# Attention's values as the stationary operand, in two parts side by side, with the transposed probabilities moving in two parts

## The chip, the cores and the metric

The kernel runs on one core of a Trainium2 chip. The metric is the device time of one execution in microseconds (us), and the median of several executions is compared. The core's engines run side by side, each in its own program order: TensorE (PE; its weight loads are listed apart as PEld), VectorE (DVE), ScalarE (ACT), GpSimd (POOL), and SyncE (SP), which here only issues transfers. They wait for one another by semaphores. On-chip memory is SBUF; TensorE writes to PSUM, in banks of 128 partitions x 512 float32 values.

## What is computed

One layer of a decoder trunk for 1024 tokens of width 1024: a spatial gating unit on one half of the projected columns, sparse attention on the other half (8 query heads of 64 in 2 groups, one key/value head for each group), an output projection `w_out` and a feed-forward part. In attention an indexer scores all earlier keys, the best 256 for each query are kept, and the change concerns what is done with them:

```
score = sum_h w_idx * relu(q_idx . k_idx)          # causal
_, idx = top_k(score, 256);  kg, vg = k[idx], v[idx]
logits = einsum('btkgd,btjkd->btkgj', qg, kg) / 8
p = softmax(logits)                                 # float32
o = einsum('btkgj,btjkd->btkgd', p, vg)
merged = concat(RMSNorm(y_a), RMSNorm(o));  x += gate * RMSNorm(merged @ w_out)
```

## The kernel before, in words

Tokens stand in 8 blocks of 128. The kernel doesn't gather keys: a mask `BI` with a large number at each key that is not kept is added to the logits of all causal keys, so query block b works on b+1 key blocks.

Most large products work in three terms: a float32 operand is split into a high part in a replicated float32 format (F32R in the code, fp32r in the trace) and a low part, the difference, in the same format. `split_w` does this for weights: ScalarE copies (and scales, L224) the high part, and VectorE (L225) or GpSimd (L222) subtracts it for the low part. `q_stack` (L391, L392) and `merge_T` (L712, L713) do it for transposed queries and for the merged rows. Products in plain F32 need no split: the transposes against `ident`, and before the change the product of probabilities and values.

The program has stages. Stage 2 projects keys, values and the indexer's vectors for each block; the values are copied by ScalarE from PSUM into `VV` (L377). Then come the indexer's scores `SC`, the gating unit (tiles `gvb`, `WM`, `vn`, `ya` in the pool `up`, together with `uv`, which the masks later use too), and the search for each query's threshold: `select(b)` is a serial chain on VectorE (L603, L605, L607), whose last step `more` (L650) releases a small matmul (L652) and, behind it on TensorE, the remaining query projections.

Attention runs over 32 units (b, group, pair of heads), blocks in the order 0, 7, 1, 6, 5, 4, 3, 2, four units for each. For unit u the loop writes, in this order: `logits(u+1)`: for each of the two heads and each chunk of up to 512 keys two matmuls (L730), one VectorE step that adds the mask and takes the minimum (L731), and one ScalarE exponential (L734) into `L`. Then `values(u)`: for each pair of key blocks (a "chunk"; 80 in all) four 128x128 transposes of `L` into one PSUM bank (`probs_T`, L769), one ScalarE copy to SBUF (`pT`, 128x512 or, for a single key block, 128x256; L750), and for each key block and head a matmul (L755) with the transposed probabilities (128x128) stationary and the 64 columns of `VV` moving. Each such matmul leaves two records in the trace. After the second pair `normed` multiplies the bank by the reciprocal of the softmax sums (L779, L780) into `yb`. Then a mask where one is due (`MASKS`: blocks 6, 5, 4, 3, 2 at units 4, 6, 8, 9, 10; block 7's before), `stack_for` the queries of unit u+3, and, four units behind, `finish` (RMSNorm of `yb`, L785, L787, and its `merge_T`). At unit 14 the first half of `w_out` is loaded through the two buffers `raw` of the pool `rp` (L207) and split; from unit 19 on, each odd unit runs `oproj0`, 24 matmuls (L807 to L809) for one finished block. adaLN sums (L481) run between on VectorE.

A scheduler decides each engine's order from the order of the code, priorities, and estimated readiness; the compiled program fixes it. Pools are stacks: memory of a pool that is closed is given to the next one, whose first writers wait for the last users.

## Time and profile before

| | us |
|---|---|
| three runs | 1246.74, 1246.16, 1245.63 (median 1246.16) |
| the profiled execution, its own time | 1248.28 |
| its span, first to last instruction | 1246.4 |
| TensorE busy in the span | 1164.5 (93%) |
| VectorE, ScalarE, GpSimd busy | 873.8, 671.2, 209.4 |
| attention, from block 7's first logits to its end | 345.5 to 546 |
| the mean granted clock of TensorE | 0.967 of full speed |

The profile is one execution. The busy shares tell which engine is full on the whole; windows tell it for a stretch; the timeline lists instructions with their starts, and the difference between two starts in a full stretch is what an instruction really takes (matmuls overlap, so their lengths are longer than their pace). A wait is given as who waited for whom.

### The profile page before, as it was taken

The page shows a single profiled execution, that of the slowest core. Times are in us where ns is not written, and L with a number is a line of the kernel's source. Part 1 is how long each engine was busy: PE and PEld are TensorE (multiplying, and loading weights), DVE is VectorE, ACT ScalarE, POOL GpSimd, SP SyncE. Part 2 cuts the span into 40 slices and gives each one's busy share as a digit, 9 for nine tenths or more (in the row PEclk, how much of TensorE's full clock was granted, in tenths as well). Part 3 has the DMA queues.
Part 4 walks back from the last instruction along what each step waited for, and adds up shares of the span by engine and source line. Part 5 has one row for each costly group of instructions (what it writes and reads, how often), then busy time and mean ns, then how long its engine had stood idle before and what let it go on. Part 6 is the DMA issues. An engine that isn't in the chain of part 4 may idle for free.

```text
span 1246.4 us, 16883 instructions
## 1 busy us (share of the span) xinstructions
PE 1164.5 (93%) x5785; PEld 985.0 (79%) x5785; DVE 873.8 (70%) x1798; ACT 671.2 (54%) x1410; POOL 209.4 (17%) x304
## 2 busy tenths in 40 slices
PE   4899989995898999899899999999999999999997
PEld 4887768884697999887687788888887888888886
DVE  7844998968478666627898775655558756876568
ACT  4554679773266755537735455555544454445452
POOL 3585605451100000012610000000000000000001
PEclk9899989996898999999999999999999999999999
DMA  9431102110000144446315753544458455533335
GB/s 343 150 93 35 52 1 64 52 64 9 1 10 29 57 161 161 172 149 215 115 60 195 269 178 127 169 143 145 161 217 331 125 188 179 197 91 99 102 98 205
DMA packets 80239, 162.41 MB, mean 130 GB/s; under 512 B 7724, under 2 KB 32920, under 8 KB 80152
## 3 DMA queue, kind: packets, MB, share of 16 engines
q1 hardware_dynamic: 80136, 161.33, 38.3%
q8 instruction: 45, 0.74, 0.3%
q14 instruction: 42, 0.34, 0.1%
q10 hardware_dynamic: 16, 0.00, 0.0%
HBM read 119.36 MB, written 41.94 MB: 129 GB/s over the span
## 4 chain that ended last, share of the span: by engine, by line
PE 51%; DVE 12%; issue 4%; DMA 3%; ACT 2%; POOL 1%; SPq 0%; DVEq 0%; POOLq 0%; ACTq 0%
PE tr L1174 8%; PE lg L1174 8%; PE mm L1174 5%; PE mm L755 4%; PE lg L991 2%; PE lg L993 2%; PE lg L992 2%; PE tr L769 2%; PE lg L730 2%; PE tr L991 2%; PE tr L993 2%; PE tr L992 2%; DVE w L882 2%; PE mm L991 1%; PE mm L993 1%
## 5 line engine op out<-in xcount | busy, mean ns | idle before, releaser
L881 ACT ACTIVATE w<-rx 128x512 fp32r<-128x512 f32 x112 | 70.7, 632 | 148.1 <-PE lg L1174 64.5
L1174 PE MATMUL tr<-w,w 128*128 128x512 f32 x504 | 134.3, 392 | 2.9 <-DVE w L882 2.9
L1174 PE MATMUL lg<-w,w 128*128 128x512 f32 x504 | 133.7, 390 | 0.0
L882 DVE TENSOR_TENSOR w<-rx,w 128x512 fp32r<-128x512 f32 x112 | 77.2, 689 | 57.8 <-ACT w L881 57.1
L301 PE MATMUL mm<-w,hT 128*128 128x512 f32 (+1 forms) x288 | 112.8, 393 | 4.7 <-ACT hT L293 3.5
L1174 PEld LDWEIGHTS tr<-w,w 128*128 128x128 f32 x504 | 95.4, 189 | 23.2 <-DVE w L882 3.4
L303 PE MATMUL mm<-w,hT 128*128 128x512 f32 (+1 forms) x288 | 111.2, 387 | 0.0
L304 PE MATMUL mm<-w,hT 128*128 128x512 f32 (+1 forms) x288 | 110.2, 384 | 1.0 <-POOL hT L294 1.0
L1174 PEld LDWEIGHTS lg<-w,w 128*128 128x128 f32 x504 | 94.9, 188 | 19.7
L1210 POOL TENSOR_TENSOR rsf<-rsf,mhalf 128x1 f32<-128x1 f32 x8 | 6.0, 752 | 605.6 <-DVE rsf L1209 605.6
L1174 PE MATMUL mm<-w,w 128*128 128x512 f32 x336 | 93.9, 389 | 0.0
L755 PEld LDWEIGHTS mm<-VV,pT 128*128 128x128 f32 x576 | 76.1, 199 | 3.8 <-ACT pT L750 1.6
L755 PE MATMUL mm<-VV,pT 128*128 128x64 f32 x576 | 76.4, 277 | 0.9 <-ACT pT L750 0.9
L1174 PEld LDWEIGHTS mm<-w,w 128*128 128x128 f32 x336 | 63.1, 188 | 13.2
L882 DVE TENSOR_TENSOR w<-b,w 128x512 fp32r<-128x512 f32 x96 | 65.7, 685 | 4.0 <-ACT w L881 4.0
L301 PEld LDWEIGHTS mm<-w,hT 128*128 128x128 f32 x288 | 55.8, 194 | 14.9 <-ACT hT L293 3.7
L730 PE MATMUL lg<-KS,qs 128*128 128x512 f32 (+5 forms) x192 | 55.3, 399 | 10.6 <-DVE mxs L731 6.0
L882 DVE TENSOR_TENSOR w<-s,w 128x512 fp32r<-128x512 f32 x56 | 38.2, 688 | 37.3 <-ACT w L881 37.3
L304 PEld LDWEIGHTS mm<-w,hT 128*128 128x128 f32 x288 | 55.0, 191 | 10.5 <-POOL hT L294 1.3
L734 ACT ACTIVATE L<-L,mxs 128x128 f32<-128x128 f32 (+7 forms) x64 | 49.2, 771 | 25.8 <-DVE mxs L731 25.6
L881 ACT ACTIVATE w<-b 128x512 fp32r<-128x512 f32 x96 | 59.4, 618 | 6.7 <-DMA b<-in_w_ff_dram 6.5
L303 PEld LDWEIGHTS mm<-w,hT 128*128 128x128 f32 x288 | 55.5, 193 | 8.5
(356 smaller groups left out, 2975.5 us busy)
## 6 DMA issues: line engine op xcount, KB each, us to landing
rx<-x_scratch SPq DMA_DIRECT2D x56, 512.0 KB, 3.5
x_scratch<-d SPq DMA_DIRECT2D x108, 256.0 KB, 3.0
ada<-in_w_ada_dram SPq DMA_DIRECT2D x48, 512.0 KB, 5.6
raw<-in_w_ff_dram SPq DMA_DIRECT2D x32, 512.0 KB, 4.1
b<-in_w_ff_dram SPq DMA_DIRECT2D x32, 512.0 KB, 4.6
x<-in_x_dram SPq DMA_DIRECT2D x16, 512.0 KB, 5.6
raw<-in_w_in_dram SPq DMA_DIRECT2D x8, 512.0 KB, 3.6
raw<-in_w_in_dram SPq DMA_DIRECT2D x16, 256.0 KB, 2.8
```

The lines of the kernel that those rows point to most:

```text
L301: mm = T.matmul(p[:, :n], lh, wt[k][:, 0, :n], start=k == 0, stop=False)
L303: T.matmul(p[:, :n], lh, wt[k][:, 1, :n], start=False, stop=False)
L304: T.matmul(p[:, :n], ll, wt[k][:, 0, :n], start=False, stop=k == KD - 1)
L730: T.matmul(pl, QS[b, grp][:, q, h4 * P:(h4 + 1) * P], KS[:, grp, c0:c0 + cw], start=q == 0, stop=q == 1)
L734: ex = A.activation(L, L, AF.Exp, scale=-1.0, bias=top, accum_out=sms[:, b, h:h + 1])
L755: mm = T.matmul(po[:, o:o + 64], e[:, (si * 2 + h2) * P:(si * 2 + h2 + 1) * P], VV[:, s0 + si, grp], start=first, stop=pair == 1 and s0 + ...
L881: A.activation(hi, src, AF.Copy)
L882: eng.tensor_tensor(lo, src, hi.bitcast(F32), op=OP.subtract)
L991: ms.append(T.matmul(p, a[:, 0, k], b[:, 0, k], start=start and k == 0, stop=False, skip_group_check=more))
L992: ms.append(T.matmul(p, a[:, 0, k], b[:, 1, k], start=False, stop=False, skip_group_check=more))
L993: ms.append(T.matmul(p, a[:, 1, k], b[:, 0, k], start=False, stop=stop and k == 3, skip_group_check=more))
L1174: ms.append(T.matmul(p, x[:, qa, t * P:(t + 1) * P], y[:, qb], start=start and n == 0, stop=stop and n == 2, skip_group_check=more))
```

## The change

Four things change; the new lines are numbered as in the file after.

1. **The product.** `VV` holds each head's 64 values twice side by side: the high part and the low part, both F32R (ScalarE copies the first, a new VectorE subtraction the second, eight times in stage 2). In `values` these 128 columns are now the stationary operand, and the transposed probabilities move: 256 columns (two heads) at a time, once their high part and once their low part. A key block and unit now take two matmuls (L768) where they took two of another shape with two records each. The result is transposed (rows: high-part and low-part outputs; columns: queries).
2. **The low part of the probabilities.** ScalarE's copy from PSUM gives the high part. The low part is subtracted by VectorE from PSUM (L764; 46 chunks), or, where `on_pool` says so (34 chunks), ScalarE copies the bank a second time into a `raw` buffer of `rp` (L759, L760) and GpSimd subtracts (L761).
3. **Back to rows.** `values_T` copies a block and group's bank to SBUF (ScalarE, `oT`, 16 times), transposes it with four TensorE transposes (L787), and `normed` first adds the two parts (a VectorE reduction from 512 to 256 elements, L806), then multiplies (L807, in place of L780). It is called one unit later, and `finish` moves one unit later too.
4. **Memory.** Two temporaries of the rotary tables reuse one buffer each; the gating unit's tiles get a pool `gp` that closes after the query projections; the probabilities' tiles take its place (pool `pe`) and from unit 13 on lie in the pool `op`, over `SC`. `mxs` loses a dimension: the first chunk's minimum is kept in `sms`.

```diff
-    VV = mid.tile([P, NB, 2, 64], F32, name="VV")
+    VV = mid.tile([P, NB, 2, P], F32R, name="VV")
...
-        A.activation(VV[:, j], vv, AF.Copy)
+        A.activation(VV[:, j, :, 0:64], vv, AF.Copy)
+        V.tensor_tensor(VV[:, j, :, 64:128], vv, VV[:, j, :, 0:64].bitcast(F32), op=OP.subtract)
...
-    gvb = up.tile([P, 512], F32, name="gvb")
+    gp_stack, gp = push("gp")
+    gvb = gp.tile([P, 512], F32, name="gvb")
...
+    gp_stack.close()
+    pe_stack, pe_pool = push("pe")
+    pe = [pe_pool]
...
-        po = PO[b, grp]
+        po = PO[b, grp][:, pair * 256:pair * 256 + 256]
...
-            e = p2.tile([P, 512], F32, tag="pT", name=nm("pT"), bufs=2)
             wd = cnt_s * 256
-            A.activation(e[:, :wd], pt[:, :wd], AF.Copy)
+            e = pe[0].tile([P, 2, 512], F32R, tag="pT", name=nm("pT"), bufs=2)
+            hi, lo = e[:, 0, :wd], e[:, 1, :wd]
+            if on_pool(u, s0):
+                r = rp.tile([P, 2, 512], F32, tag="raw", name=nm("pr"))[:, 0, :wd]
+                A.activation(r, pt[:, :wd], AF.Copy)
+                A.activation(hi, pt[:, :wd], AF.Copy)
+                G.tensor_tensor(lo, r, hi.bitcast(F32), op=OP.subtract)
+            else:
+                A.activation(hi, pt[:, :wd], AF.Copy)
+                V.tensor_tensor(lo, pt[:, :wd], hi.bitcast(F32), op=OP.subtract)
             for si in range(cnt_s):
-                for h2 in range(2):
-                    o = (pair * 2 + h2) * 64
...
-                    mm = T.matmul(po[:, o:o + 64], e[:, (si * 2 + h2) * P:(si * 2 + h2 + 1) * P], VV[:, s0 + si, grp],
-                                  start=first, stop=pair == 1 and s0 + si == ns - 1 and h2 == 1)
+                for q in range(2):
...
+                    mm = T.matmul(po, VV[:, s0 + si, grp], e[:, q, si * 256:si * 256 + 256], start=first,
+                                  stop=pair == 1 and s0 + si == ns - 1 and q == 1)
...
-        if pair == 1:
-            normed(yb_of(b)[:, grp * 256:grp * 256 + 256].rearrange("p (h e) -> p h e", h=4),
-                   po[:, :256].rearrange("p (h e) -> p h e", h=4), b, grp * 4, 4)
+
+    def on_pool(u, s0):
+        b = units[u][0]
+        if b < 2:
+            return False
+        return (s0 // 2) % 2 == 0 if b > 5 else s0 == 0 if b == 5 else u % 4 < 2
+
+    def values_T(b, grp):
+
+        oT = p2.tile([P, 512], F32, tag="yb", name=nm("oT"), bufs=3)
+        A.activation(oT, PO[b, grp], AF.Copy)
+        p = p_tr()
+        for i in range(4):
+            T.transpose(p[:, i * P:(i + 1) * P], oT[:, i * P:(i + 1) * P], ident)
+        normed(yb_of(b)[:, grp * 256:grp * 256 + 256].rearrange("p (h e) -> p h e", h=4),
+               p.rearrange("p (h w e) -> p h e w", h=4, w=2), b, grp * 4, 4)
...
         V.reciprocal(sms[:, b, h:h + n], sms[:, b, h:h + n])
-        V.tensor_tensor(dst, src, sms[:, b, h:h + n, None].to_broadcast([P, n, 64]), op=OP.mult)
+        V.tensor_reduce(dst, src, op=OP.add, axis=mybir.AxisListType.X)
+        V.tensor_tensor(dst, dst, sms[:, b, h:h + n, None].to_broadcast([P, n, 64]), op=OP.mult)
...
+        if u and u % 2 == 0:
+            values_T(*units[u - 1][:2])
         values(u)
         if u in MASKS:
             mask(MASKS[u])
         if u == 12:
+            pe_stack.close()
             u_stack.close()
             sc_stack.close()
             o_stack, op_ = push("op")
+            pe[0] = op_
...
-        if u % 4 == 0 and u:
+        if u % 4 == 1 and u > 1:
             finish(OB[u // 4 - 1])
...
+    values_T(OB[-1], 1)
     finish(OB[-1])
```

VectorE in stretch A, from the mask of block 4's end into block 3's; before (the names: `self`, `seli`, `eq` belong to the mask, `mT` is the merged rows, `L` the logits):

```order
L671 CAST seli_2643<-self_2642 128x1
L674 SCALAR_TENSOR_TENSOR seli_2643<-seli_2643 128x1
L676 TENSOR_TENSOR self_2642<-seli_2643,self_2642 128x1
L680 TENSOR_SCALAR BI,self_2642<-SC,self_2642 128x512
L713 TENSOR_TENSOR mT_4154<-tr_4270,mT_4154 128x4x128
L681 TENSOR_SCALAR eq_4306<-SC,self_2642 128x512
L683 TENSOR_SCALAR self_2642<-self_2642 128x1
L731 ISA L_4324,mxs<-lg_4325,BI 128x256
```

After, at the mask of block 3 (lines are shifted by some 5: L679 is the former L674, L681 L676, L685 L680, L686 L681, L688 L683, L718 L713, L822 L795):

```order
L806 TENSOR_REDUCE yb_4424<-tr_4419 128x256
L718 TENSOR_TENSOR mT_4220<-tr_4398,mT_4220 128x4x128
L679 SCALAR_TENSOR_TENSOR seli_2657<-seli_2657 128x1
L764 TENSOR_TENSOR pT_4434<-tr_4429,pT_4434 128x512
L822 TENSOR_SCALAR ya_4452<-ya_4452,rsa 128x512
L807 TENSOR_TENSOR yb_4424<-yb_4424,sms 128x256
L681 TENSOR_TENSOR self_2656<-seli_2657,self_2656 128x1
L685 TENSOR_SCALAR BI,self_2656<-SC,self_2656 128x512
L686 TENSOR_SCALAR eq_4375<-SC,self_2656 128x512
L688 TENSOR_SCALAR self_2656<-self_2656 128x1
L718 TENSOR_TENSOR mT_3147<-tr_4458,mT_3147 128x4x128
```

Between the steps of the same mask now stand a subtraction (L764), a reduction (L806) and the product with the sums (L807).

ScalarE where the first half of `w_out` is scaled; before:

```order
L750 ACTIVATE pT_4463<-tr_4458 128x512
L734 ACTIVATE L_4493,sms<-L_4493,mxs 128x896
L750 ACTIVATE pT_4472<-tr_4469 128x256
L224 ACTIVATE wo_4642<-raw_4640,cols 128x512
L224 ACTIVATE wo_4645<-raw_4640,cols 128x512
L224 ACTIVATE wo_4650<-raw_4648,cols 128x512
L224 ACTIVATE wo_4653<-raw_4648,cols 128x512
L712 ACTIVATE mT_3122<-tr_4486 128x4x128
```

After:

```order
L759 ACTIVATE pr_4746<-tr_4740 128x512
L760 ACTIVATE pT_4745<-tr_4740 128x512
L763 ACTIVATE pT_4757<-tr_4754 128x256
L717 ACTIVATE mT_4220<-tr_4768 128x4x128
L224 ACTIVATE wo_4777<-raw_4775,cols 128x512
L224 ACTIVATE wo_4780<-raw_4775,cols 128x512
L224 ACTIVATE wo_4785<-raw_4783,cols 128x512
L224 ACTIVATE wo_4788<-raw_4783,cols 128x512
L224 ACTIVATE wo_4793<-raw_4791,cols 128x512
L224 ACTIVATE wo_4796<-raw_4791,cols 128x512
L759 ACTIVATE pr_4833<-tr_4827 128x512
```

Four scalings of two loads stood in a row and the other four came one pair at a time; now six of three loads stand in a row, directly behind a chunk whose second copy `pr` takes a `raw` buffer, and ahead of the next one.

TensorE in stretch B, in block 5's values; before:

```order
L755 MATMUL mm_4896<-VV,pT_4968 128x64 x4
L755 MATMUL mm_4896<-VV,pT_4979 128x64 x4
L769 MATMUL tr_4985<-ident,L_4876 128x128
L769 MATMUL tr_4985<-ident,L_4886 128x128
L769 MATMUL tr_4985<-ident,L_4876 128x128
L769 MATMUL tr_4985<-ident,L_4886 128x128
L322 MATMUL tr_5001<-ident,qd_4999 128x128 x4
L730 MATMUL lg_5049<-KS,qs_4866 128x320
```

After (L795 is the former L769, L835 the former L808):

```order
L795 MATMUL tr_5137<-ident,L_5034 128x128
L768 MATMUL mm_5065<-pT_5071,VV 128x256 x3
L768 MATMUL mm_5065<-pT_5085,VV 128x256 x4
L795 MATMUL tr_5137<-ident,L_5044 128x128
L795 MATMUL tr_5137<-ident,L_5034 128x128
L795 MATMUL tr_5137<-ident,L_5044 128x128
L835 MATMUL mm_5185<-wo_4801,mT_3147 128x512
```

Four matmuls for a pair of key blocks stay four, with the values as second operand; transposes of the next chunk and the output projection's matmuls stand between a chunk's first matmul and its others.

## Rows read from the trace of the kernel before

**Rows 1.** The page, busy time, share of the span and instructions of each engine.
```profile
PE 1164.5 (93%) x5785; PEld 985.0 (79%) x5785; DVE 873.8 (70%) x1798; ACT 671.2 (54%) x1410; POOL 209.4 (17%) x304
```

**Rows 2.** Windows: start:end, length, then busy us (instructions) per engine, clock, DMA, GB/s.
```profile
345.50:399.40 53.90, 49.94 (x376) 46.58 (x375) 49.17 (x139) 35.12 (x75) 5.18 (x10) 0.94 0.02 6
399.40:546.00 146.60, 141.00 (x982) 130.28 (x981) 90.29 (x207) 85.95 (x189) 9.95 (x14) 0.97 0.39 137
```

**Rows 3.** The same view, windows of 4 us in stretch A.
```profile
372.00:376.00 4.00, 3.25 (x27) 2.90 (x25) 3.75 (x14) 2.47 (x10) 0.00 (x0) 1.00 0.00 0
376.00:380.00 4.00, 1.48 (x9) 1.51 (x10) 3.86 (x10) 1.05 (x3) 0.55 (x1) 0.87 0.00 0
380.00:384.00 4.00, 4.00 (x19) 3.66 (x18) 4.00 (x12) 2.56 (x7) 0.77 (x1) 0.50 0.00 0
```

**Rows 4.** Timeline of VectorE (start, us, line, operation) in stretch A.
```profile
375.38 1.48 DVE L682 TENSOR_TENSOR_SCAN SC<-eq 128x640 f32<-128x640 bf16 x1
...
377.89 0.48 DVE L787 TENSOR_SCALAR yb<-yb,rsb 128x512 f32<-128x512 f32 x1
```

**Rows 5.** Waits in stretch A: who waited for whom, us in total, times, longest.
```profile
PE tr L709 <- DVE yb L787: 2.9, 1, 2.9
```

**Rows 6.** Timeline of TensorE; xN is a run of N records without another between.
```profile
371.70 0.60 PE L769 MATMUL tr<-ident,L 128*128 128x128 f32 x4
372.14 1.00 PE L755 MATMUL mm<-VV,pT 128*128 128x64 f32 x8
372.95 0.96 PE L730 MATMUL lg<-KS,qs 128*128 128x256 f32 x6
373.74 1.00 PE L755 MATMUL mm<-VV,pT 128*128 128x64 f32 x8
...
411.48 1.89 PE L755 MATMUL mm<-VV,pT 128*128 128x64 f32 x16
413.19 0.94 PE L730 MATMUL lg<-KS,qs 128*128 128x384 f32 x4
```

**Rows 7.** Timeline of VectorE, instructions that follow one another without a gap.
```profile
374.63 0.42 DVE L731 CUSTOM_DVE_ANT_0 L<-lg,BI 128x256 f32<-128x256 f32 x1
374.97 0.09 DVE L731 DVE_READ_ACCUMULATOR2_ANT mxs<- 128x1 f32 x1
...
449.04 0.69 DVE L392 TENSOR_TENSOR qs<-tr,qs 128x512 fp32r<-128x512 f32 x1
449.64 0.42 DVE L780 TENSOR_TENSOR yb<-mm,sms 128x256 f32<-128x256 f32 x1
```

**Rows 8.** Groups by line and shape, ScalarE, 340 to 546 us: count | busy, mean ns.
```profile
L750 ACT ACTIVATE pT<-tr 128x512 f32<-128x512 f32 x64 | 37.3, 592 | 15.2 <-PE tr L769 10.3 <-PE mm L755 4.7
```

**Rows 9.** Groups by line, GpSimd, 0 to 345 us.
```profile
L222 POOL TENSOR_TENSOR w<-raw,w 128x512 fp32r<-128x512 f32 (+1 forms) x40 | 51.2, 1300 | 15.1 <-ACT w L221 7.6 <-DMA x<-in_x_dram 5.8 <-PE mm L304 1.3
```

**Rows 10.** w_out, first half: timeline of ScalarE.
```profile
398.30 2.56 ACT L224 ACTIVATE wo<-raw,cols 128x512 fp32r<-128x512 f32 x4
...
404.78 1.33 ACT L224 ACTIVATE wo<-raw,cols 128x512 fp32r<-128x512 f32 x2 [1.45 <-DMA raw<-in_w_out_dram]
```

**Rows 11.** The page, DMA issues: KB each, us from issue to landing.
```profile
raw<-in_w_in_dram SPq DMA_DIRECT2D x8, 512.0 KB, 3.6
```

**Rows 12.** Timeline of ScalarE, w_out, second half.
```profile
522.82 2.55 ACT L224 ACTIVATE w<-raw,cols 128x512 fp32r<-128x512 f32 x4
...
530.92 1.34 ACT L224 ACTIVATE w<-raw,cols 128x512 fp32r<-128x512 f32 x2 [2.58 <-DMA raw<-in_w_out_dram]
```

**Rows 13.** Timeline of TensorE at the end of the search.
```profile
310.12 0.19 PE L652 MATMUL tr<-ones,more 128*1 128x1 f32 x2 [9.48 <-DVE more L650]
```

**Rows 14.** Timeline of VectorE (two rows) and of GpSimd (the last).
```profile
372.40 0.15 DVE L674 SCALAR_TENSOR_TENSOR seli<-seli 128x1 int32<-128x1 int32 x1
...
389.19 0.60 DVE L674 SCALAR_TENSOR_TENSOR seli<-seli 128x1 int32<-128x1 int32 x1
...
389.17 0.62 POOL L388 COPY qd<-q 128x512 f32<-128x512 f32 x1 [7.35 <-PE tr L322]
```

More of the change, by code (lines that the diff above doesn't have):

```diff
@@ L236, in rotary @@
     def rotary():
-        posf = t0.tile([8, P], F32, name="posf")
+        posf = posr.bitcast(F32)
         V.tensor_copy(posf, posr)
@@ L247, in rotary @@
         for i, (turn, add) in enumerate(((0.25, math.pi / 2), (0.0, 0.0))):
-            n_ = t0.tile([P, 64], F32, name=nm("n"))
+            n_ = t0.tile([P, 64], F32, tag="rn", name=nm("n"), bufs=1)
             a_ = ang.rearrange("p a b -> p (a b)")
@@ L252, in rotary @@
             V.tensor_scalar(n_, n_, MAGIC, None, op0=OP.subtract)
-            r_ = t0.tile([P, 64], F32, name=nm("r"))
+            r_ = t0.tile([P, 64], F32, tag="rr", name=nm("r"), bufs=1)
             V.scalar_tensor_tensor(r_, n_, -c1, a_, op0=OP.mult, op1=OP.add)
@@ L411, in trunk @@
                     channel_multiplier=1)
-    WM = up.tile([P, 4, P], F32, name="WM")
+    WM = gp.tile([P, 4, P], F32, name="WM")
     pw = p_tr()
@@ L518, in gate_in @@
         ge = A.activation(uv, p, AF.Gelu_apprx_tanh)
-        vn = up.tile([P, 2, P], F32, tag="vn", name=nm("vn"), bufs=2)
+        vn = gp.tile([P, 2, P], F32, tag="vn", name=nm("vn"), bufs=2)
         ss = ssv[:, j, 2 * cc:2 * cc + 2]
@@ L534, in gate_out @@
         pg = p_tr()
-        ya = up.tile([P, 2, P], F32, tag="ya", name=nm("ya"), bufs=1)
+        ya = gp.tile([P, 2, P], F32, tag="ya", name=nm("ya"), bufs=1)
         for i in range(2):
@@ L699, in trunk @@
     rsb = ct([P, NB], F32, "rsb")
-    mxs = ct([P, 2, NB, 8], F32, "mxs")
+    mxs = ct([P, NB, 8], F32, "mxs")
     sms = ct([P, NB, 8], F32, "sms")
@@ L730, in logits @@
                     T.matmul(pl, QS[b, grp][:, q, h4 * P:(h4 + 1) * P], KS[:, grp, c0:c0 + cw], start=q == 0, stop=q == 1)
+                m = (mxs if i == len(ch) - 1 else sms)[:, b, h:h + 1]
                 lowest[0] = V.tensor_tensor_reduce(L[:, c0:c0 + cw], pl, bias[:, c0:c0 + cw], scale=-0.125, scalar=top,
-                                       op0=OP.add, op1=OP.min, accum_out=mxs[:, i, b, h:h + 1])
-                top = mxs[:, i, b, h:h + 1]
+                                       op0=OP.add, op1=OP.min, accum_out=m)
+                top = m
             ex = A.activation(L, L, AF.Exp, scale=-1.0, bias=top, accum_out=sms[:, b, h:h + 1])
@@ L747, in values @@
             pt = probs_T(u, s0, cnt_s)
-            e = p2.tile([P, 512], F32, tag="pT", name=nm("pT"), bufs=2)
             wd = cnt_s * 256
-            A.activation(e[:, :wd], pt[:, :wd], AF.Copy)
-            for si in range(cnt_s):
-                for h2 in range(2):
-                    o = (pair * 2 + h2) * 64
-                    first = pair == 0 and s0 + si + h2 == 0
-                    mm = T.matmul(po[:, o:o + 64], e[:, (si * 2 + h2) * P:(si * 2 + h2 + 1) * P], VV[:, s0 + si, grp],
-                                  start=first, stop=pair == 1 and s0 + si == ns - 1 and h2 == 1)
+            e = pe[0].tile([P, 2, 512], F32R, tag="pT", name=nm("pT"), bufs=2)
[8 more added lines that the diff above has]
+                V.tensor_tensor(lo, pt[:, :wd], hi.bitcast(F32), op=OP.subtract)
+            for si in range(cnt_s):
+                for q in range(2):
+                    first = pair == 0 and s0 + si + q == 0
+                    mm = T.matmul(po, VV[:, s0 + si, grp], e[:, q, si * 256:si * 256 + 256], start=first,
+                                  stop=pair == 1 and s0 + si == ns - 1 and q == 1)
                     if first:
```

## The prediction

> **What bounds the kernel now.** I began with the page's busy shares: TensorE is busy 93% of the span, VectorE 70%, ScalarE 54%, GpSimd 17% [rows 1]. Such a share mixes stages, so I cut the span where the change works. It touches attention alone, 345 to 546 us; the later 700 us run the same instructions in the same order before and after. Attention falls in two stretches [rows 2]. In **A**, 345.5 to 399.4 us, from the first logits of query block 7 to just after the last mask, TensorE is busy 49.9 of 53.9 us, but so is VectorE, 49.2: it searches, masks and corrects, and has 4.7 us to spare. In **B**, 399.4 to 546 us, TensorE is busy 141 of 146.6 us and VectorE 90, ScalarE 86: there TensorE is the bound.
>
> That VectorE really sets the pace in A is read from small windows: in 372 to 384 us it is busy 11.6 of 12 us [rows 3]. At 375.38 it runs a scan of 1.48 us, then other mask steps, and only at 377.89 the scaling of yb [rows 4] for which TensorE idles 2.9 us [rows 5]. The granted clock then falls: 1.00 in 372 to 376, 0.87, and 0.50 in 380 to 384, the lower of its two levels [rows 3]. So a wait of 2.9 us is paid twice.
>
> **The change part by part.** *Values on TensorE.* Eight records of 128x64 (one pair of key blocks) run from 372.14 to 372.95, sixteen from 411.48 to 413.19: 0.107 us each [rows 6]. A has 184 of them and B 376: 19.7 and 40.2 us. The change replaces four such records by two matmuls, each of 256 columns in the replicated format. The nearest row is the logits' 256 columns, six from 372.95 to 373.74, 0.132 us each [rows 6]. So A 92 x 0.132 = 12.1 and B 188 x 0.132 = 24.8 us. The outputs now come out transposed and cost four transposes (0.11 us each by the four from 371.70 to 372.14, [rows 6]) per block and group: 5 in A, 10 in B, +2.2 and +4.4. Net: **A -5.4, B -11.0 us of TensorE**.
>
> Here a rule of the Trainium skill speaks against the change. Its page "FP8 and Floating Point Precision", section "TensorE Precision Notes", says that true FP32 takes four passes through the array; two matmuls of 64 columns would then stream 512 columns per key block, and the new pair streams 512 too, so only the transposes would be left and the sum below would be about 15 us higher (B's 40.2 - 24.8). The rows have 0.43 us per key block against 0.26, so here something else than columns paces the narrow ones.
>
> *The low halves on VectorE.* Of 80 chunks, 46 get a subtraction on VectorE. Its nearest rows read PSUM and SBUF as it will: 128x512 starts at 449.04 and the next instruction at 449.64, 0.60 us; a 256-wide one takes 0.34 from start to start (374.63 to 374.97) [rows 7]. The order of the changed program puts 13 full and 2 half ones, and 5 new reductions (512 elements from PSUM, unknown: between 0.34 and 0.60; I take 0.60, since they read as many elements), between the same two marks in A: 7.8 + 0.7 + 3.0 = **+11.5 us on VectorE in A**. In B stand 21 full, 7 half and 10 reductions: 12.6 + 2.4 + 6.0 = **+21 us**, which gives 111.
>
> *GpSimd's chunks.* 34 chunks, 24 of them in B, get a second copy on ScalarE (0.59 us [rows 8]) and a subtraction on GpSimd, 1.30 us by the nearest row [rows 9]. B's ScalarE gains 24 x 0.59, the four half ones taken as full, + 10 x 0.59 (the transposed outputs' copies) = 20, to 106 us. A chunk's low half now comes 0.6 us (VectorE) or 0.6 + 1.3 us (a second copy, GpSimd) after its high half; the matmuls on the high half, the next transposes and logits cover this while VectorE is not late.
>
> *Sum in A.* VectorE: 49.2 + 11.5 = 60.7 us of work where there were 53.9: +6.8 if it never idles, +11.5 if its 4.7 us stay. I take **+9**, the middle. TensorE's 5.4 us disappear under it.
>
> *Sum in B.* TensorE's paced work falls by 11; its gaps stay if neither of the others is late. VectorE would be at 111 and ScalarE at 106 of 135 us, each in program order. I take 2 us for that: **-9** (-11 to 0).
>
> *w_out's loads.* The GpSimd chunks borrow the two raw buffers into which w_out is loaded. Before, the first two loads lay in them long ahead: four scalings at 398.3 needed no load, and only the later loads made ScalarE wait 1.4 us [rows 10]. Now every load stands behind a GpSimd subtraction, and six scalings in a row stand on ScalarE ahead of the next probabilities' copies, six corrections in a row on VectorE. The nearest load of this size takes 3.6 us from issue to landing [rows 11]; the second pair waits for the corrections of the first, so there are two such waits: 7.2 us, less some 3 us of copies queued ahead and the 1.4 of before, makes 2.8. The same comes again at 523 us, where the first four scalings need no wait and the next wait 2.6 us already [rows 12]; little is added there. Bounds 0 (all covered) and 10 (three loads bare); I take **+3**.
>
> *Early.* At 309.9 us TensorE waits 9.5 us for VectorE's search [rows 13]. Block 0's three half subtractions and its reduction now stand in that queue ahead: 3 x 0.34 + 0.60 = **+1.6** (0 to 3).
>
> *Small ones.* The eight 128x128 subtractions for the values' low halves fall where VectorE has gaps, as does the rotary tables' reuse of buffers: **+0.5** (0 to 1; at most 8 x 0.34 = 2.7 if those gaps are taken). The probabilities' tiles move to a pool that from unit 13 on lies over the scores, and so wait for the last mask: in A's price already. The pool of the gating tiles costs no instruction.
>
> **Sum:** 1.6 + 0.5 + 9 + 3 - 9 = **+5.1 us**. The profiled execution took 1248.28 us, 1246.4 of it span; its changed time would be 1253.4. The median of the runs shown is 1246.16, 2.1 below: **1251.3**.
>
> **The rivals.** *Faster.* The masks are not what TensorE waits for in A: the one long wait named there is 2.9 us, and it is busy 93% [rows 2, 5]. Then the added VectorE work pushes the masks back into B, where VectorE has 56 idle us, and TensorE's saving is kept in both. Price: -5.4 - 11 + 1.6 + 3 = -12, some 1234; with half of A's push, +4.5 in the place of -5.4 and the rest equal, near 1244; so 1239 as the middle of it. Against it: the blocks' logits need their masks, and windows with VectorE full [rows 3]. It decides if at the marks of A's end VectorE's 60.7 us have not made the stretch longer than 56 us.
>
> *No change.* The sum's terms A and B are of a size: with A at +7, w_out at 1 and B at -10 the rest is 0: 1246.
>
> *Slower than the sum: GpSimd holds VectorE up.* At 389.17 a GpSimd copy of 0.62 us starts, and a VectorE step of 128x1 takes 0.60 instead of 0.15 us and ends with it [rows 14]. The change adds 34 x 1.3 = 44 us of GpSimd, 31 of them in B. If a third of these meet a VectorE step that is held for half their length, that is 24 / 3 x 0.65 = 5 us on VectorE in B and 2 in A; B's gain then goes to 0 as ScalarE and VectorE take turns in making TensorE wait and the clock falls as at 380 us: 1.6 + 0.5 + 11.5 + 2 + 4 + 0 = +20, 1266.
>
> The Trainium skill has the rule for it, page "SBUF — State Buffer", section "Who interferes with whom": GpSimd and VectorE share a port pair by exclusive lock, and VectorE contends in its two-port modes or with two SBUF inputs. By that rule the new VectorE subtractions, with one input in PSUM, would not be held, but the masks, the adaLN sums and the scalings would; the row at 389.17 agrees that such a hold exists.
>
> **How the numbers follow.** About 0.2% (2.5 us) is what a measurement of this kernel can tell from no change. Forecast (+2.5 to +12): 0.45. Slower than that, GpSimd or coupling in B: 0.13, of which 0.02 for narrow matmuls that were no dearer than the wide ones (+20). Within 2.5 us: 0.17. Faster: 0.25. That makes faster 0.25, same 0.17, slower 0.58. The range leaves out a tenth on each side: 1237 (most of the faster case) to 1264 (most of the slower one).
>
> **What would show it.** In the changed profile: the values' matmuls at 0.13 us each, 288 of them; the stretch from block 7's first logits to the last mask's end 60 to 65 us long with VectorE above 93% busy; B some 137 us with TensorE below 95%; ScalarE's waits for w_out's first loads 3 us longer; the wait for the search near 11 us. I am wrong if A stays under 56 us (then faster), if B stays at 146 us (then 1260 and more), or if VectorE's subtractions take over 0.8 us a piece beside GpSimd.

## The result: 4.4% slower

The changed kernel took 1299.22 us (median of four runs, 1297.65 to 1303.61), the kernel before 1245.89 us in the same comparison. The ratio is 1.044, with a 95% interval of 1.041 to 1.047. The forecast said slower, but by 5 us, and its range ended at 1264. The direction was right and the size was wrong by a factor of ten.

The page of the changed kernel, busy time of each engine (before: [rows 1]):

```profile
PE 1173.3 (90%) x5561; PEld 972.5 (75%) x5561; DVE 923.9 (71%) x1868; ACT 697.1 (54%) x1460; POOL 256.7 (20%) x338
```

TensorE's busy share fell from 93% to 90%, GpSimd's rose from 17% to 20%. The profiled execution took 1298.92 us, its span is 1297.2. Three events of the trace cut it into stretches that every kernel of this study has: the start of the last query projection's matmul, the start of the last mask's last step, and the start of the last matmul of the output projection's first half. Between the first two lies stretch A, between the last two stretch B. In us:

| kernel | start to last query projection | A | B |
|---|---|---|---|
| before | 344.2 | 54.1 | 153.0 |
| changed | 351.0 | 71.7 | 180.3 |
| difference | +6.8 | +17.6 | +27.3 |

The rest differs by 1 us. The two stretches as windows of the changed kernel (columns as in [rows 2]):

```profile
351.00:422.70 71.70, 54.51 (x313) 44.59 (x311) 65.66 (x159) 43.86 (x92) 19.69 (x21) 0.90 0.03 8
422.70:603.00 180.30, 153.89 (x863) 128.78 (x863) 120.55 (x248) 104.38 (x226) 45.50 (x39) 0.91 0.36 121
```

In A VectorE has 65.7 us of work where [rows 2] had 49.2 (a window of the same work, some 1 us off at either end), and TensorE idles for 17 of 72 us. In B VectorE has 120.6 us and ScalarE 104.4, both far from full, and yet TensorE is busy only 154 of 180 us, at a granted clock of 0.91 where it was 0.97. So in B no engine is full: the time went into waits of one for another and into a lower clock. TensorE's longest waits in B, who for whom, us in total, times, longest:

```profile
PE lg L735 <- DVE sms L737: 10.0, 3, 8.3
PE mm L768 <- ACT pT L763: 3.9, 3, 2.8
PE tr L787 <- ACT oT L784: 3.5, 4, 1.6
PE mm L768 <- POOL pT L761: 2.7, 3, 1.4
```

The largest single one is where the first half of `w_out` is loaded. Timelines of TensorE, ScalarE and VectorE there (start, length, instruction, idle time before it and what ended it):

```profile
439.87 0.60 PE L795 MATMUL tr<-ident,L 128*128 128x128 f32 x4
448.77 1.01 PE L735 MATMUL lg<-KS,qs 128*128 128x384 f32 x2 [8.30 <-DVE sms L737]
```

```profile
440.20 1.33 ACT L224 ACTIVATE wo<-raw,cols 128x512 fp32r<-128x512 f32 x2 [1.59 <-DMA raw<-in_w_out_dram]
443.01 1.33 ACT L224 ACTIVATE wo<-raw,cols 128x512 fp32r<-128x512 f32 x2 [1.48 <-DMA raw<-in_w_out_dram]
446.07 1.33 ACT L224 ACTIVATE wo<-raw,cols 128x512 fp32r<-128x512 f32 x2 [1.72 <-DMA raw<-in_w_out_dram]
448.33 0.60 ACT L759 ACTIVATE pr<-tr 128x512 f32<-128x512 f32 x1 [0.93 <-DVE wo L225]
```

```profile
438.64 0.69 DVE L718 TENSOR_TENSOR mT<-tr,mT 128x512 fp32r<-128x512 f32 x1
440.95 1.43 DVE L225 SCALAR_TENSOR_TENSOR wo<-raw,cols,wo 128x512 fp32r<-128x512 f32 x2 [1.62 <-ACT wo L224]
443.76 1.41 DVE L225 SCALAR_TENSOR_TENSOR wo<-raw,cols,wo 128x512 fp32r<-128x512 f32 x2 [1.38 <-ACT wo L224]
446.82 1.42 DVE L225 SCALAR_TENSOR_TENSOR wo<-raw,cols,wo 128x512 fp32r<-128x512 f32 x2 [1.64 <-ACT wo L224]
448.15 0.55 DVE L737 CUSTOM_DVE_ANT_0 L<-lg,BI 128x384 f32<-128x384 f32 x1
```

Three pairs of scalings on ScalarE each wait 1.5 to 1.7 us for a load, VectorE's corrections (L225) follow pair by pair, and the next logits' step (L737, for which TensorE waits 8.3 us) and the next probabilities' copies (L759) stand behind all of them. Before, the first four scalings had their loads ahead [rows 10]. Two windows of 8 us show the stop and what follows it:

```profile
440.00:448.00 8.00, 0.47 (x5) 0.23 (x3) 4.02 (x6) 4.00 (x6) 0.00 (x0) 0.64 0.61 191
448.00:456.00 8.00, 6.20 (x28) 5.48 (x29) 6.05 (x18) 6.35 (x13) 3.10 (x3) 0.72 0.01 5
```

TensorE is busy 0.47 of 8 us, and in the next 8 us the granted clock is 0.72: part of the work after a stop runs at the lower level, 1.2 GHz, as it did at 380 us before [rows 3].

### The profile page after: what moved, and what is told of

It reads as the page before. It is cut to its first block, busy times and chain, and to the rows that moved or that the text cites. A ratio compares the mean times of both kernels' runs of the same rounds, so it can differ in the third digit from the quotient of the medians.

```text
span 1297.2 us, 16612 instructions
## 1 busy us (share of the span) xinstructions
PE 1173.3 (90%) x5561; PEld 972.5 (75%) x5561; DVE 923.9 (71%) x1868; ACT 697.1 (54%) x1460; POOL 256.7 (20%) x338
## 4 chain that ended last, share of the span: by engine, by line
PE 53%; DVE 13%; ACT 3%; DMA 3%; issue 2%; POOL 1%; SPq 0%; DVEq 0%; POOLq 0%; ACTq 0%
PE tr L1206 8%; PE lg L1206 8%; PE mm L1206 5%; PE lg L1023 3%; PE lg L1025 3%; PE lg L1024 3%; PE tr L1023 2%; PE tr L1025 2%; PE tr L1024 2%; PE mm L834 2%; PE mm L835 2%; PE mm L836 2%; DVE L L737 2%; PE mm L1023 2%; PE mm L1024 2%
## 5 line engine op out<-in xcount | busy, mean ns | idle before, releaser
L301 PE MATMUL mm<-w,hT 128*128 128x512 f32 (+1 forms) x288 | 114.5, 399 | 8.6 <-ACT hT L293 7.3
L303 PE MATMUL mm<-w,hT 128*128 128x512 f32 (+1 forms) x288 | 112.8, 392 | 0.5 <-DVE self L622 0.4
L304 PE MATMUL mm<-w,hT 128*128 128x512 f32 (+1 forms) x288 | 111.5, 388 | 0.3 <-POOL hT L294 0.3
L768 PE MATMUL mm<-pT,VV 128*128 128x256 f32 x288 | 64.3, 332 | 19.1 <-DVE pT L764 7.0
L735 PE MATMUL lg<-KS,qs 128*128 128x512 f32 (+5 forms) x192 | 57.9, 404 | 25.5 <-DVE sms L737 16.6
L768 PEld LDWEIGHTS mm<-pT,VV 128*128 128x128 f32 x288 | 48.0, 214 | 31.3 <-DVE pT L764 10.3
L301 PEld LDWEIGHTS mm<-w,hT 128*128 128x128 f32 x288 | 56.5, 196 | 19.9 <-ACT hT L293 7.4
L761 POOL TENSOR_TENSOR pT<-pr,pT 128x512 fp32r<-128x512 f32 (+1 forms) x34 | 45.9, 1356 | 113.0 <-ACT pT L760 106.7
L303 PEld LDWEIGHTS mm<-w,hT 128*128 128x128 f32 x288 | 56.6, 197 | 9.9 <-POOL w L222 1.4
L304 PEld LDWEIGHTS mm<-w,hT 128*128 128x128 f32 x288 | 56.1, 195 | 10.0 <-POOL hT L294 0.6
```

Of the source, the lines that this page charges most:

```text
L301: mm = T.matmul(p[:, :n], lh, wt[k][:, 0, :n], start=k == 0, stop=False)
L303: T.matmul(p[:, :n], lh, wt[k][:, 1, :n], start=False, stop=False)
L304: T.matmul(p[:, :n], ll, wt[k][:, 0, :n], start=False, stop=k == KD - 1)
L735: T.matmul(pl, QS[b, grp][:, q, h4 * P:(h4 + 1) * P], KS[:, grp, c0:c0 + cw], start=q == 0, stop=q == 1)
L761: G.tensor_tensor(lo, r, hi.bitcast(F32), op=OP.subtract)
L768: mm = T.matmul(po, VV[:, s0 + si, grp], e[:, q, si * 256:si * 256 + 256], start=first, stop=pair == 1 and s0 + si == ns - 1 and q == 1)
```

## The experiments

Each was timed in turn with the kernel before on the same chip, and the ratios are to those runs; not all were timed on the same chip. The line under each diff is the text on record from before the run. Each run is a program of its own, for which the scheduler can choose another order of the instructions that are left, so a difference between two runs holds that too.

**Without the low halves.** In `values`:

```diff
-            if on_pool(u, s0):
-                ...
             A.activation(hi, pt[:, :wd], AF.Copy)
-                V.tensor_tensor(lo, pt[:, :wd], hi.bitcast(F32), op=OP.subtract)
...
-                    mm = T.matmul(po, VV[:, s0 + si, grp], e[:, q, si * 256:si * 256 + 256], start=first,
+                    mm = T.matmul(po, VV[:, s0 + si, grp], e[:, 0, si * 256:si * 256 + 256], start=first,
```

> The changed kernel without the low halves of the probabilities: no subtraction on VectorE or GpSimd, no second copy, nothing in the raw buffers; both matmuls of a key block take the high half, so the output lacks the low part and counts the high one twice. TensorE's work is that of the change. If the low halves' making is what costs the 53 us (theory), about 1240: the 7 us of the early stages stay, some 12 us of TensorE are gained. If the product itself and its transposed output cost (rival), it stays above 1270.

Measured: 1253.83 us, ratio 1.006 (1.004 to 1.009). So the making of the low halves, the buffers that it takes and the waiting for it are 3.8% of the 4.4. But it is not the 1240 of the theory: what is left of the change, the product that was to save TensorE's time included, is still 0.6% slower than the kernel before.

**All low halves on VectorE.** `on_pool` returns False for every block.

> All 80 subtractions on VectorE, none on GpSimd, no second copies, the raw buffers free for w_out's loads. If GpSimd's chunks are the larger cost (GpSimd holding VectorE up, late low halves, loads of w_out behind them): 1275 or less although VectorE gets 20 us more. If VectorE's own added work is what costs: 1305 to 1320.

Measured: 1278.68 us, ratio 1.027 (1.024 to 1.030). The theory that GpSimd's chunks cost more than half was right in direction: with 34 more subtractions on VectorE, 20 us of work, the kernel gets 20 us faster, since GpSimd's subtractions, ScalarE's second copies and the shared raw buffers go, all at once. It missed the 1275 by 4 us.

**Without GpSimd's subtractions, second copies kept.**

```diff
-                G.tensor_tensor(lo, r, hi.bitcast(F32), op=OP.subtract)
...
-                    mm = T.matmul(po, VV[:, s0 + si, grp], e[:, q, si * 256:si * 256 + 256], start=first,
+                    mm = T.matmul(po, VV[:, s0 + si, grp], e[:, 0 if on_pool(u, s0) else q, si * 256:si * 256 + 256], start=first,
```

> Only GpSimd's 34 subtractions are left out (those chunks take their high half twice, so the output lacks their low part); second copies on ScalarE and the raw buffers stay. If GpSimd's operations cost by holding VectorE and by their lateness: 1275 or less. If VectorE's subtractions cost: 1288 or more, since only some 9 us of holds go.

Measured: 1278.56 us, ratio 1.025 (1.022 to 1.029). It lies between the text's two marks, 1275 and 1288. 34 instructions on an engine that is busy a fifth of the time cost 1.9%, some 23 us.

**GpSimd's subtractions made, but read by nobody.** Only the second half of the diff above.

> The changed kernel, in which GpSimd makes its 34 low halves as before but no matmul reads them (those chunks take the high half twice, so the output lacks their low part). If TensorE's waiting for GpSimd's late low halves is what those subtractions cost: 1283 or less, near the run without them (1278.6). If it is GpSimd holding VectorE up and the buffers that it keeps: 1293 or more.

Measured: 1286.57 us, ratio 1.034 (1.030 to 1.038). It lies between the two theories. TensorE's waiting for GpSimd's late low halves is 1.0% (from 1.034 to the changed kernel's 1.044), and what GpSimd does to others without being waited for by the matmuls is 0.8% (from 1.025 to 1.034). So the 23 us are two costs of about 10 to 13 us, each uncertain by some 0.5%, or 6 to 7 us. The stretches show what they consist of (A and B of the run without the subtractions, then of the run in which nobody reads them; each B window ends 0.1 to 0.7 us before its mark):

```profile
353.30:416.60 63.30, 50.58 (x317) 41.36 (x315) 59.47 (x160) 43.38 (x93) 7.05 (x11) 0.97 0.03 9
416.60:575.00 158.40, 140.50 (x856) 121.02 (x857) 111.40 (x247) 103.20 (x225) 10.72 (x15) 0.96 0.40 137
```

```profile
352.20:419.90 67.70, 51.36 (x317) 41.30 (x315) 63.84 (x160) 43.81 (x93) 22.23 (x21) 0.97 0.03 9
419.90:589.00 169.10, 145.82 (x858) 125.31 (x859) 120.22 (x247) 104.12 (x226) 48.78 (x39) 0.93 0.38 128
```

Unread, the subtractions make A 4.4 us longer, just what VectorE is busy longer there. In B VectorE is busy some 9 us longer and the stretch is some 10 longer, but there TensorE's longest wait, at w_out's scalings, grows too, from 5.3 to 8.6 us, and one of 4.6 us for the scaling of ya is new; the holding of VectorE and the buffers that GpSimd keeps aren't separated in B. When the matmuls read the low halves, A and B together grow by 15 us more, of which 4 are idle time of TensorE and 11 are its own busy time for the same work: the granted clock is 0.90 and 0.91 in the changed kernel's A and B, 0.97 and 0.93 here. How much of the 11 is the clock and how much is matmuls that overlap less isn't separated.

**Second copies out of the raw buffers.**

```diff
-                r = rp.tile([P, 2, 512], F32, tag="raw", name=nm("pr"))[:, 0, :wd]
+                r = wp.tile([P, 1024], F32, tag="w", name=nm("pr"))[:, :wd]
```

> The second copies lie in the pool of weights and logits instead of the two raw buffers, so w_out's first loads run ahead again, as before the change. The gap of TensorE at 440 to 448 us and the half clock behind it should go: 1287 to 1290 (10 us) if the loads are one cost among several; 1270 or less if they were the main one; unchanged if another wait takes their place.

Measured: 1291.76 us, ratio 1.038 (1.034 to 1.041): some 8 us (uncertain by 6) faster than the changed kernel, one cost among several, though 2 us above the 1287 to 1290 that stood for that. The new place of the copies is shared with weights and logits and can cost waits of its own. ScalarE now waits for the first loads 2.1 us once, and the wait of 8.3 us is gone. What TensorE waits for most from 420 to 591 us in this run (who for whom, us in total, times, longest):

```profile
PE tr L787 <- ACT oT L784: 5.2, 7, 1.1
PE mm L768 <- POOL pT L761: 4.9, 3, 2.3
```

The first is the way of the outputs back to rows, the second GpSimd's low halves.

**Without the second copies as well.** In the run without GpSimd's subtractions, the copy into `pr` is left out too.

> The run without GpSimd's subtractions, and its 34 second copies on ScalarE left out too: 46 chunks with low halves from VectorE, 34 with the high half twice (the output lacks their low part). If the copies' 20 us on ScalarE are on the path: 1262 to 1266 in the place of 1278.6. If ScalarE has room for them and VectorE's 46 subtractions are the rest of the price: 1273 or more.

Measured: 1266.71 us, ratio 1.017 (1.013 to 1.022). The copies and the two raw buffers that they take cost 0.8%, some 10 us (uncertain by 7), although ScalarE is busy only 54% of the span. The two causes go together here, since without the copies w_out's loads run ahead again. TensorE's wait for the logits' step behind w_out's scalings, with the copies and then without:

```profile
PE lg L735 <- DVE sms L737: 6.4, 3, 5.3
```

```profile
PE lg L735 <- DVE sms L737: 1.8, 2, 1.0
```

So the stop at w_out comes with the copies even where GpSimd subtracts nothing, and its 4.6 us of added waiting are about half of the 10; what ScalarE's 20 us of work cost by themselves is then less, and not measured. No run has the copies elsewhere and no subtraction.

**High half once.** The run without low halves, with one matmul for each key block (`for q in range(1)`).

> The changed kernel with one matmul for each key block, on the high half alone; no low half of the probabilities is made or used (the output lacks it). Against the run without low halves TensorE has 144 matmuls of 0.13 us less, 12 us of them in stretch B. If TensorE bounds B once the low halves are gone: 1240 to 1244. If it is bound by the chain from the transposes over ScalarE and back: 1250 or more.

Measured: 1244.72 us, ratio 0.999 (0.997 to 1.001). It stands within 1 us of the text's 1240 to 1244. 144 matmuls less are worth 0.7%, 9 us, nearly all in B (141.8 us against 151.3, where 12.4 us of matmuls went). So TensorE's time does count in B, at about three quarters.

**No way back to rows.** The run without low halves, and in `values_T`:

```diff
-        oT = p2.tile([P, 512], F32, tag="yb", name=nm("oT"), bufs=3)
-        A.activation(oT, PO[b, grp], AF.Copy)
-        p = p_tr()
-        for i in range(4):
-            T.transpose(p[:, i * P:(i + 1) * P], oT[:, i * P:(i + 1) * P], ident)
+        p = PO[b, grp]
```

> The run without low halves, and the outputs' way back to rows left out too: no copy of the bank, no four transposes; the reduction and the product with the sums read the bank as it is, so the output is not in its order. TensorE has 64 transposes (7 us) and ScalarE 16 copies (9 us) less. If the way back is what eats TensorE's gain in stretch B (the chain bank, ScalarE, transposes, VectorE, then the merge): 1242 to 1246, 8 or more below the 1253.8 with it. If TensorE's saved time in B is covered by other waits anyway: 1250 or more.

Measured: 1240.90 us, ratio 0.994 (0.993 to 0.996). The way back costs 1.15%, 14 us, for 7 us of transposes and 9 us of copies. B as a window, first with the way back (it ends 0.2 us before the mark), then without:

```profile
402.30:553.40 151.10, 141.22 (x877) 123.35 (x877) 98.86 (x227) 96.08 (x210) 12.55 (x16) 0.97 0.40 137
```

```profile
401.10:538.60 137.50, 130.56 (x814) 116.13 (x814) 96.24 (x220) 87.83 (x193) 10.48 (x15) 0.97 0.44 151
```

TensorE is busy 10.7 us less, with 63 records less, and the stretch is 13.6 us shorter. Without the way back, B is 137.5 us, 15.5 less than before, and the forecast's saving of the product itself was 15.4: the product gave about what its rows promised, and the way back took most of it. Where it stands in the run with it, as waits in B:

```profile
PE tr L780 <- ACT oT L777: 3.1, 3, 2.1
PE mm L761 <- ACT pT L757: 2.9, 2, 2.2
```

Three of B's ten sets of four transposes wait for ScalarE's copy of the bank, which stands in ScalarE's queue behind other work (for 2.1 us at 414.8, behind an exponential and a copy of the merge); while they wait, what follows them on TensorE waits too. These waits are 3 of the 13.6 us, and the transposes themselves 7; where the other 3 or 4 us of TensorE's busy time come from isn't traced.

**The early parts alone,** on the kernel before: eight subtractions into a tile that nobody reads, and the rotary tables' reuse of buffers, to which belongs that the positions are converted in place.

```diff
-        posf = t0.tile([8, P], F32, name="posf")
+        posf = posr.bitcast(F32)
...
-            n_ = t0.tile([P, 64], F32, name=nm("n"))
+            n_ = t0.tile([P, 64], F32, tag="rn", name=nm("n"), bufs=1)
...
-            r_ = t0.tile([P, 64], F32, name=nm("r"))
+            r_ = t0.tile([P, 64], F32, tag="rr", name=nm("r"), bufs=1)
...
         A.activation(VV[:, j], vv, AF.Copy)
+        vlo = t0.tile([P, 2, 64], F32, tag="vlo", name=nm("vlo"), bufs=1)
+        V.tensor_tensor(vlo, vv, VV[:, j], op=OP.subtract)
```

> The kernel before with the early parts of the change alone: the eight subtractions for the values' low halves (into a tile that nobody reads) and the rotary tables' reuse of buffers. If the 7 us by which the changed kernel is late at the indexer's first scores come from these and are not absorbed: 1251 to 1253. If they are absorbed by the search: 1246 to 1248.

Measured: 1254.09 us, ratio 1.008 (1.005 to 1.011). Some 10 us by the ratio, and not absorbed. The traces, one execution each, show less: this run is 4.5 us late at the start of the last query projection's matmul and 3.0 at B's end. Each part by itself (the positions are converted in place in both):

> The kernel before with the rotary tables' reuse of buffers alone. If the second table, which now waits for the first one's sine, delays everything behind it: most of the 8 us of the early parts, 1252 or more. If the subtractions of the values do it: 1246 to 1248.

Measured: 1244.25 us, ratio 1.001 (0.999 to 1.003).

> The kernel before with the eight subtractions for the values' low halves alone (into a tile that nobody reads). If they stand in VectorE's queue ahead of what TensorE waits for at 67 to 75 us: 1252 or more. If the rotary tables do it: 1246 to 1248.

Measured: 1248.85 us, ratio 1.004 (1.002 to 1.006). The subtractions cost something by themselves, 0.4%, between the two sizes of the text; the buffers nothing that is clear; together they cost more than the sum, 0.8 against 0.5%, though the intervals meet. Waits of TensorE in the first 110 us, before and then in the changed kernel:

```profile
PE mm L301 <- ACT hT L293: 3.5, 2, 2.2
...
PE tr L322 <- POOL kv L317: 1.7, 1, 1.7
```

```profile
PE mm L301 <- ACT hT L293: 7.3, 2, 6.0
PE tr L322 <- POOL kv L317: 4.6, 2, 2.5
```

The first wait is as long in the run with the rotary buffers alone (7.3 us), the second in the run with the subtractions alone (4.3 us). So each part lengthens another wait. Why only both together delay the stage's end isn't settled.

**Both operands rounded, nothing else,** on the kernel before:

```diff
-    VV = mid.tile([P, NB, 2, 64], F32, name="VV")
+    VV = mid.tile([P, NB, 2, 64], F32R, name="VV")
...
-            e = p2.tile([P, 512], F32, tag="pT", name=nm("pT"), bufs=2)
+            e = p2.tile([P, 512], F32R, tag="pT", name=nm("pT"), bufs=2)
```

> The kernel before with values and probabilities rounded to the replicated format and nothing else changed: the same stationary and moving operands, no low halves at all (the product loses them). If each matmul then leaves one record of the same 0.107 us: 288 x 0.107 = 31 us less for TensorE, 20 of them in stretch B, 10 in A where VectorE is full: 1224 to 1230. If 64 columns are no cheaper in that format: 1246.

Measured: 1233.09 us, ratio 0.990 (0.987 to 0.994): faster than both kernels, at the price of the low halves' precision. The time lies between the text's two. The records halve in number and nearly keep their pace; four from 401.73 to 402.20, 0.117 us each:

```profile
401.73 0.63 PE L755 MATMUL mm<-VV,pT 128*128 128x64 f32 x4
402.20 0.66 PE L769 MATMUL tr<-ident,L 128*128 128x128 f32 x4
```

Of 31 us of TensorE's work, 12 came out as time. B fell from 153.0 to 139.7 us, A from 54.1 to 51.7. What is late next in attention is ScalarE's copy of the probabilities, for which TensorE waited 0.9 us before and now:

```profile
PE mm L755 <- ACT pT L750: 6.9, 10, 2.0
```

## Why the prediction was wrong, point by point

The ratios form a chain from the kernel before to the changed one, each step one part added; the parts of the change that no step names (its pools, the later `finish`, the reductions) stand in the second. It adds up by construction; each link is uncertain by some 0.3 to 0.6%. Beside it stands the same by the traces, one execution each: how much later B ends than in the run of the step before.

| step | ratio after it | us of 1246 | B's end, us | the forecast's term |
|---|---|---|---|---|
| early parts | 1.008 | +10 | +3.0 | +0.5 |
| product, without the way back | 0.994 | -17 | -15.7 | -15.4 in B; in A +3 of VectorE for reductions |
| the way back to rows | 1.006 | +14 | +15.0 | +4.4 of TensorE in B |
| 46 subtractions on VectorE | 1.017 | +14 | +14.4 | +1.6 before A, +8.5 in A; 2 us of gaps in B |
| 34 second copies on ScalarE, into w_out's buffers | 1.025 | +10 | +7.7 | none for the copies, +3 for w_out |
| GpSimd's 34 subtractions, unread | 1.034 | +10 | +13.4 | holds only in a rival |
| TensorE's waiting for them | 1.044 | +13 | +13.9 | none |

The scheduler's order isn't the same along the chain: between the run in which nobody reads them and the changed kernel some 50 of VectorE's 403 instructions in A and B stand elsewhere in the order, between the runs without and with the second copies some 70 of 407, and without and with GpSimd's subtractions some 20. What of a step is due to the order wasn't measured.

**The amounts of work were right.** The forecast had 111 us for VectorE and 106 for ScalarE in B. The run without GpSimd's subtractions and second copies has 112.0 for VectorE (window of its B), and the changed kernel 104.4 for ScalarE. The new matmuls were to take 0.132 us; four of them, from 465.65 to 466.23, take 0.145 each. First that window, then TensorE's timeline:

```profile
413.20:568.00 154.80, 144.16 (x871) 124.93 (x870) 111.98 (x250) 94.07 (x206) 13.67 (x16) 0.96 0.39 134
```

```profile
465.65 0.74 PE L768 MATMUL mm<-pT,VV 128*128 128x256 f32 x4
466.23 0.72 PE L735 MATMUL lg<-KS,qs 128*128 128x384 f32 x3
```

**A was right for what it counted.** With VectorE's share of the low halves alone (no second copies, nothing on GpSimd) A is 61.2 us; the forecast's +9 would have been 63. The changed kernel's 71.7 has 10 us more, and they are GpSimd's chunks: 63.3 with the copies, 67.7 with the unread subtractions, 71.7 with TensorE waiting for them.

**The step that failed is "TensorE's paced work falls by 11; its gaps stay if neither of the others is late ... I take 2 us for that".** B was to gain 9 us and lost 27.3; from run to run along the chain it is 154.1, 137.5, 151.3, 154.8, 159.1, 169.2 and 180.3 us long, so VectorE's 46 subtractions took 3.5 us of it, near the 2, and the way back, the second copies with w_out's loads, and GpSimd's chunks took the rest. The step treated VectorE and ScalarE as late only when full, and had no term for the clock behind a wait, though the prediction had seen at 380 us that a wait is paid twice. By the program, B is a ring of small steps instead: transposes, a copy on ScalarE, a subtraction on VectorE or GpSimd, matmuls, and two buffers of probabilities that close the ring. Each step added to the ring waits its turn in a queue that also holds masks, exponentials, adaLN sums of 1.3 us and w_out's corrections. That price was between half the length of the added instructions (GpSimd's subtractions, 46 us long, 23) and nearly the whole (the way back, 16 us long, 14). VectorE's and ScalarE's busy shares, 67% and 58% in B, said nothing of it. What is shown is the price of each step; that the two buffers are what ties the steps together is argued, for no run had more of them. "Slower than the sum" was a rival with 1266 and 0.13 (0.02 of it for narrow matmuls); it named the right mechanisms, GpSimd's holds and the taking of turns, and priced them at little more than a third.

**"The matmuls on the high half, the next transposes and logits cover this while VectorE is not late"** was the second step that failed. TensorE runs in its own order, and a matmul on a late low half stops all that is behind it: 13 us for GpSimd's chunks, most of it, as shown above, as busy time at a lower clock. For VectorE's chunks the condition itself failed in A; the waits for their low halves there, in the changed kernel:

```profile
PE mm L768 <- DVE pT L764: 6.7, 4, 2.2
```

**GpSimd's holds** were priced at 7 us in the rival and at nothing in the sum. VectorE in A (first fence), with GpSimd's subtractions at the same places (second):

```profile
354.90 1.25 DVE L679 SCALAR_TENSOR_TENSOR seli<-seli 128x1 int32<-128x1 int32 x1
...
379.49 2.76 DVE L687 TENSOR_TENSOR_SCAN SC<-eq 128x768 f32<-128x768 bf16 x1
...
382.48 1.98 DVE L690 SCALAR_TENSOR_TENSOR eq<-SC,self,eq 128x768 bf16<-128x768 f32 x1
```

```profile
354.83 1.30 POOL L761 TENSOR_TENSOR pT<-pr,pT 128x512 fp32r<-128x512 f32 x1 [0.66 <-ACT pT L760]
...
379.36 1.28 POOL L761 TENSOR_TENSOR pT<-pr,pT 128x512 fp32r<-128x512 f32 x1 [2.05 <-ACT pT L760]
382.38 1.27 POOL L761 TENSOR_TENSOR pT<-pr,pT 128x512 fp32r<-128x512 f32 x1 [1.75 <-ACT pT L760]
```

The step of 128x1 at 354.90 ends with GpSimd's subtraction, 1.25 us for 0.15. The scan at 379.49 takes 2.76 us, as long as the rest of GpSimd's instruction (1.15) and the 1.75 that it takes in the run without GpSimd's subtractions, less a little. Groups of VectorE in attention, in the changed kernel and then in the run without GpSimd's subtractions:

```profile
L483 DVE SCALAR_TENSOR_TENSOR adacc<-ada,cact,adacc 128x1024 f32<-128x1024 f32 x21 | 31.4, 1497 | 0.3
L764 DVE TENSOR_TENSOR pT<-tr,pT 128x512 fp32r<-128x512 f32 x34 | 23.0, 682 | 11.8 <-ACT pT L763 11.8
L718 DVE TENSOR_TENSOR mT<-tr,mT 128x512 fp32r<-128x512 f32 x15 | 10.3, 686 | 19.5 <-ACT mT L717 19.4
...
L690 DVE SCALAR_TENSOR_TENSOR eq<-SC,self,eq 128x896 bf16<-128x896 f32 x1 | 2.1, 2060 | 0.0
...
L679 DVE SCALAR_TENSOR_TENSOR seli<-seli 128x1 int32<-128x1 int32 x5 | 1.8, 365 | 0.0
```

```profile
L483 DVE SCALAR_TENSOR_TENSOR adacc<-ada,cact,adacc 128x1024 f32<-128x1024 f32 x21 | 27.1, 1293 | 0.9 <-DMA ada<-in_w_ada_dram 0.8
L763 DVE TENSOR_TENSOR pT<-tr,pT 128x512 fp32r<-128x512 f32 x34 | 23.1, 682 | 6.9 <-ACT pT L762 6.7
L718 DVE TENSOR_TENSOR mT<-tr,mT 128x512 fp32r<-128x512 f32 x15 | 10.3, 685 | 12.7 <-ACT mT L717 12.7
...
L687 DVE TENSOR_TENSOR_SCAN SC<-eq 128x768 f32<-128x768 bf16 x1 | 1.7, 1748 | 0.0
...
L690 DVE SCALAR_TENSOR_TENSOR eq<-SC,self,eq 128x896 bf16<-128x896 f32 x1 | 1.2, 1152 | 0.0
...
L679 DVE SCALAR_TENSOR_TENSOR seli<-seli 128x1 int32<-128x1 int32 x5 | 0.7, 146 | 0.0
```

The adaLN sums (L483) lose 0.20 us each, 21 times; the mask's comparison of 128x896 (L690) takes 2.06 against 1.15. Over all groups the difference of mean length times count is 13 us on VectorE, and 12 with the subtractions unread, where the kernel pays 10 by the ratio. What reads one operand from PSUM (L764, L718) is not touched: 682 and 682 ns, 686 and 685.

The rule that the prediction cited as a rival's, from the Trainium skill, page "SBUF — State Buffer", section "Who interferes with whom", says of instructions with two SBUF inputs that they contend with GpSimd's reads. The trace agrees in both halves: where those above met a GpSimd subtraction they were held up to its end, and those with an input in PSUM were not. The scalings of yb, whose one tensor lies in SBUF, were held too (0.73 against 0.60 us, mean of 8); the prediction had the scalings among the held.

**The rule on true FP32's four passes,** which the prediction cited from the Trainium skill, page "FP8 and Floating Point Precision", section "TensorE Precision Notes", and which would have put the sum 15 us higher, was rightly left out of the sum: without low halves and way back the product gained 17 us against the early parts alone. And two rounded operands of 64 columns took 0.117 us a record, near the 0.107 of before, with half the records.

**w_out's loads** were sized +3 (0 to 10) and cost 8, uncertain by 6 (1.044 against 1.038). The 8 are no step of the chain but part of its last three. The forecast had two waits with some 3 us covered. There were three, of 1.6, 1.5 and 1.7 us, with VectorE's corrections in between, and after them came the half clock.

**The early parts** were sized +0.5 and measured about 10 by the ratio, 3.0 by B's end; by neither were they hidden in VectorE's gaps. In the changed kernel the search was late by 4.7 us at its end (the last step at 314.5 against 309.8), but the indexer's first scores had been late by 7 (109.4 against 102.2). With the early parts alone the last step comes at 313.2, so most of the lateness is theirs and not block 0's. The wait for the search, which was to grow to 11 us, fell to 7.6.

**The faster rival** failed by its own sign: A was to stay under 56 us, and is 71.7. "No change" failed with B. That the forecast had the direction right rests on A, where its mechanism held; B's sign was wrong, so the direction was in part luck.

## What to carry to other kernels

Work that is moved off a busy engine onto idle ones was not free here, where the steps stand in a chain with two buffers: where a later instruction of the bottleneck stands behind them, added steps cost between half of their length and nearly all of it, whatever the receiving engine's busy share, and part of that came as a lower clock of the bottleneck. Before splitting an operand for precision's sake, time the split's own cost with the product left as it is and with the split left out: here the product gained 17 us and what it needed cost 71. And a buffer that is borrowed from a prefetch costs the prefetch.

## What the runs showed of the hardware that was not expected

A GpSimd subtraction of 1.30 us held a VectorE step of 0.15 us on 128x1 values for 1.25 us, and a long step for what was left of it; steps with an operand in PSUM ran beside it at full speed (682 ns with and without). A matmul record of 128x64 took 0.107 us in float32 and 0.117 us with rounded operands, with two records for each matmul in the first case and one in the second; so the time followed the number of records more than the format. And the waits that a late operand caused showed mostly as longer busy time: 11 of 15 us in A and B, at a granted clock of 0.90 and 0.91 in the place of 0.97 and 0.93.
